# Layer 1's modulations move from the mixer into layer 0's values, summed by row on VectorE, with one more raw buffer and weight pair

## The chip, the cores and the metric

One core of a Trainium2 chip. The metric is the device time of one launch in microseconds, the median of several runs; lower is better.

## The reference, cut to what matters

A two-layer backbone over 256 latent tokens of 1024 features, with 256 context tokens in front. Each layer has a mixer and then a PEER expert layer, each with a normalisation that six modulation vectors of 1024 shift, scale and gate:

```python
c_act = jax.nn.silu(c)
for i in range(2):
    mod = (c_act @ ada_w[i] + ada_b[i]).reshape(bsz, 6, 1, 1024)
    sh1, sc1, g1, sh2, sc2, g2 = (mod[:, j] for j in range(6))
    h = rmsnorm(x, norm1_w[i]) * (1.0 + sc1) + sh1
    y = mixer_ab(h, h_c, ...) if i == 0 else fourier_mix(h) @ w_out_f
    x = x + g1 * y
    x = x + g2 * peer(rmsnorm(x, norm2_w[i]) * (1.0 + sc2) + sh2, ...)
return rmsnorm(x, final_norm_w)
```

`ada_w[i]` is 1024 x 6144, so a layer's modulations are one vector times 25 MB of weights. Layer 0's first two vectors are also needed for the context (with `c_ctx` in place of `c`). `peer` projects to queries (`wq`, 16 tiles), finds for each token and head the top 16 of 16,384 experts by two rounds of top-16 over keys, and sums `gate * gelu(h . u[e]) * v[e]`. The kernel computes all 16,384 activations with the table `u` (128 tiles of 128 experts), sets a dense weight matrix from the chosen experts, and multiplies with the table `v` (128 tiles).

## The kernel before

**Stages.** One program: the mixer of layer 0 (0 to about 440 us), `peer` of layer 0 (queries, the 128 `u` tiles with selection and weighting beside them, then the 128 `v` tiles), the Fourier mixer of layer 1 (about 1256 to 1290), `peer` of layer 1, the final norm.

**The weight stream.** `Stream` reads every large weight in one fixed order, as tiles of 128x1024 fp32 (512 KB). `loads` takes one of three raw buffers and starts the transfer on SyncE's queue. `cuts` splits each tile into a high part (a rounded copy in fp32r by ScalarE) and a low part (raw minus high, by VectorE), after which the raw buffer is free. The two parts of a tile are a pair; there are two pairs of the stream's own, and other stages lend theirs (two in the values, one in the `u` tiles). A 256-column product then takes three matmuls a block of 128: high x high, high x low and low x high, 24 matmuls to a tile.

**The modulations.** `modulations` in `mixer` computes both layers' vectors: six parts (two layers, three each), two halves, eight blocks of 128 input channels, 96 chunks of 512 KB. A chunk is loaded into one of six buffers for the first part, of two (`mraw`) for the others, and takes four fp32 matmuls, in which the activated condition (`cact`, 32 columns) is the stationary side and 256 chunk columns are the moving side; the trace has two records for each fp32 matmul. After a part, ScalarE copies the rows out (`mrow`), four transposes turn them into columns, and VectorE adds the bias. Layer 0's first part (16 chunks) must be there before the projections can start; its gates are needed at the mixer's end, and layer 1's vectors only after `peer` of layer 0.

**The rest of the mixer.** 29 projections (`products`, 17 of 512 columns and 12 of 256), at most three in flight, convolutions, attention, and a triangular inverse as 31 dependent steps on VectorE (`inverse`). When all projections are done, their buffer is set to zero by GpSimd (`zero`), the inverse is transposed into it (`blocks`), merged and scanned.

**Selection and weighting.** `select` runs top-16 on VectorE. `weigh` builds one-hot matrices on VectorE (four fp16 operations of 128x1024 for eight tokens), multiplies them on TensorE (fp16), and `spread` multiplies the result into the activations. Both run beside the `u` tiles. In `values` the weights are split (`weights`: ScalarE copies, VectorE subtracts, 128x512 per two tiles) and multiplied with the `v` pairs into four of the eight PSUM banks.

**The order.** The program is written by a planner. Each activity is a generator; `Lanes` keeps a clock for each engine, picks the generator that is ready first, and emits its next instructions. `took` is its price list and `landed` its guess at a transfer. The engines then run their own instructions in exactly that order, with semaphores between them. Prices so decide the order, not the time. `PACE` multiplies VectorE's prices in `select` (1.35) and `weigh` (1.1).

## Time and profile before

| what | value |
|---|---|
| median of 3 runs | 2119.27 us (2117.88 to 2119.61) |
| the profiled execution | 2115.18 us |
| its span, first to last instruction | 2113.4 us |
| mean granted TensorE clock | 0.989 of full speed |
| TensorE, VectorE, ScalarE busy | 2063.5, 1549.2, 1022.1 us |
| read from memory | 366.71 MB |

PE is TensorE's matmul, PEld its weight load, DVE VectorE, ACT ScalarE, POOL GpSimd, SPq SyncE's queue. Nearly all instructions stand at line 133, the planner's call, so groups are told apart by the names of their tiles: `raw` is a raw buffer, `pair`, `wide`, `h` and `wide_lo` hold parts of pairs at different times, `mraw` and `area` hold modulation chunks, `bank` is PSUM, `S` is the projections' input and later the inverse.

### The profile page before, as it was taken

The page shows a single profiled execution, that of the slowest core. Times are in us where ns is not written, and L with a number is a line of the kernel's source. Part 1 is how long each engine was busy: PE and PEld are TensorE (multiplying, and loading weights), DVE is VectorE, ACT ScalarE, POOL GpSimd, SP SyncE. Part 2 cuts the span into 40 slices and gives each one's busy share as a digit, 9 for nine tenths or more (in the row PEclk, how much of TensorE's full clock was granted, in tenths as well). Part 3 has the DMA queues.
Part 4 walks back from the last instruction along what each step waited for, and adds up shares of the span by engine and source line. Part 5 has one row for each costly group of instructions (what it writes and reads, how often), then busy time and mean ns, then how long its engine had stood idle before and what let it go on. Part 6 is the DMA issues. An engine that isn't in the chain of part 4 may idle for free.

```text
span 2113.4 us, 43065 instructions
## 1 busy us (share of the span) xinstructions
PE 2063.5 (98%) x17732; PEld 1933.9 (92%) x17732; DVE 1549.2 (73%) x3039; ACT 1022.1 (48%) x1542; POOL 82.8 (4%) x122
## 2 busy tenths in 40 slices
PE   7999989999999999999999999999999999999998
PEld 3566658989999999999999989999999999999997
DVE  3479978879998999565555556999899956555554
ACT  4443344155545444554444545554544455444453
POOL 3000023000000000000000000000000000000000
PEclk8999999999999999999999999999999999999999
DMA  7655671045565444665655543556544466666553
GB/s 300 213 180 169 232 240 38 1 133 180 189 198 170 142 149 151 198 212 196 192 195 194 193 160 116 172 190 199 170 141 149 150 199 211 195 194 193 196 192 118
DMA packets 102549, 370.65 MB, mean 175 GB/s; under 512 B 11696, under 2 KB 12976, under 8 KB 101968
## 3 DMA queue, kind: packets, MB, share of 16 engines
q1 hardware_dynamic: 102352, 367.90, 53.0%
q8 instruction: 138, 2.26, 0.4%
q14 instruction: 59, 0.48, 0.1%
HBM read 366.71 MB, written 1.15 MB: 174 GB/s over the span
## 4 chain that ended last, share of the span: by engine, by line
PE 79%; DVE 10%; DMA 6%; ACT 3%; issue 1%; POOL 0%; SPq 0%; POOLq 0%; ACTq 0%; DVEq 0%
PE bank L133 79%; DMA raw<-in_u_dram 3%; DVE wide_lo L133 3%; DVE pair L133 2%; DVE wide L133 2%; DMA mraw<-in_ada_w_dram 2%; DVE DD L133 1%; DVE area L133 1%; ACT pair L133 1%; DMA area<-in_ctx_dram 1%; ACT wide L133 0%; ACT DD L133 0%; DMA area<-in_ada_w_dram 0%; ACT bank L133 0%; DVE a L133 0%
## 5 line engine op out<-in xcount | busy, mean ns | idle before, releaser
L133 ACT ACTIVATE pair<-raw 128x1024 fp32r<-128x1024 f32 x376 | 399.1, 1062 | 435.2 <-PE bank L133 342.9
L133 DVE TENSOR_TENSOR pair<-raw,pair 128x1024 fp32r<-128x1024 f32 x376 | 458.1, 1219 | 182.8 <-ACT pair L133 167.1
L133 PE MATMUL bank<-h,pair 128*128 128x256 f32 x4464 | 557.4, 280 | 0.0
L133 PEld LDWEIGHTS bank<-h,pair 128*128 128x128 f32 x4464 | 528.8, 188 | 0.2 <-DVE pair L133 0.2
L133 PE MATMUL bank<-wide,pair 128*128 128x256 f32 (+1 forms) x3456 | 417.1, 277 | 0.0
L133 PEld LDWEIGHTS bank<-wide,pair 128*128 128x128 f32 x3456 | 405.4, 188 | 0.6
L133 PE MATMUL bank<-wide,h 128*128 128x256 f32 x2880 | 336.6, 276 | 0.0
L133 PEld LDWEIGHTS bank<-wide,h 128*128 128x128 f32 x2880 | 331.3, 188 | 0.0
L133 PE MATMUL bank<-h,wide 128*128 128x256 f32 x2160 | 264.5, 277 | 0.0
L133 PEld LDWEIGHTS bank<-h,wide 128*128 128x128 f32 x2160 | 253.7, 188 | 0.0
L133 DVE TENSOR_TENSOR h<-raw,h 128x1024 fp32r<-128x1024 f32 x120 | 147.0, 1225 | 140.1 <-ACT h L133 140.1
L133 ACT ACTIVATE h<-raw 128x1024 fp32r<-128x1024 f32 x120 | 127.4, 1062 | 161.8 <-PE bank L133 149.2
L133 PE MATMUL bank<-S,pair 128*128 128x256 f32 (+1 forms) x888 | 195.5, 362 | 4.2 <-POOL S L133 2.5
L133 PEld LDWEIGHTS bank<-S,pair 128*128 128x128 f32 x888 | 138.8, 199 | 52.3 <-issue 29.9
L133 ACT ACTIVATE DD<-bank 128x512 f32<-128x512 f32 (+25 forms) x284 | 107.6, 394 | 95.8 <-PE bank L133 92.8
L133 ACT ACTIVATE wide<-raw 128x1024 fp32r<-128x1024 f32 x90 | 95.6, 1062 | 106.7 <-PE bank L133 53.3
L133 DVE TENSOR_TENSOR wide<-raw,wide 128x1024 fp32r<-128x1024 f32 x90 | 109.3, 1214 | 2.3 <-ACT wide L133 2.0
L133 DVE TENSOR_TENSOR wide<-DD,wide 128x512 fp32r<-128x512 f32 x128 | 87.3, 684 | 8.3 <-ACT wide L133 8.2
L133 DVE TENSOR_TENSOR DD<-bank,DD 128x512 f32<-128x512 f32 (+13 forms) x84 | 42.3, 504 | 64.8 <-ACT bank L133 61.2
L133 DVE TENSOR_TENSOR wide_lo<-wide_lo,pT 128x1024 f16<-128x1024 f16 x128 | 85.9, 681 | 0.0
L133 ACT ACTIVATE wide<-DD 128x512 fp32r<-128x512 f32 x128 | 78.6, 615 | 9.5 <-PE bank L133 9.5
L133 POOL TENSOR_TENSOR wide_lo<-wide_lo 128x256 f32<-128x256 f32 x10 | 8.3, 834 | 1591.5 <-ACT wide_lo L133 1590.9
(242 smaller groups left out, 1893.7 us busy)
## 6 DMA issues: line engine op xcount, KB each, us to landing
raw<-in_u_dram SPq DMA_DIRECT2D x256, 512.0 KB, 3.5
raw<-in_v_dram SPq DMA_DIRECT2D x256, 512.0 KB, 4.3
mraw<-in_ada_w_dram SPq DMA_DIRECT2D x84, 512.0 KB, 4.2
raw<-in_wq_dram SPq DMA_DIRECT2D x32, 512.0 KB, 3.5
raw<-in_w_in_dram SPq DMA_DIRECT2D x29, 512.0 KB, 4.3
area<-in_ada_w_dram SPq DMA_DIRECT2D x12, 512.0 KB, 6.3
raw<-in_w_out_ab_dram SPq DMA_DIRECT2D x8, 512.0 KB, 4.5
raw<-in_w_out_f_dram SPq DMA_DIRECT2D x8, 512.0 KB, 3.5
```

The source lines that it names most:

```text
L133: return f(*args, **kw)
```

## The change

- Layer 1's 48 chunks leave `modulations` in the mixer, which keeps layer 0's three parts. Their weights are laid out anew (`ada_late`: vector, block of 128 input channels, 1024 outputs).
- They enter the weight stream among layer 0's 128 `v` tiles, two chunks for five tiles from the third tile on, in the order `ADA` of the vectors. They take raw buffers but no pair.
- A chunk is multiplied by its 128 condition values (one to a partition) and added into a 128x1024 accumulator `acc` by VectorE (`sum`): one `tensor_scalar`, then seven `scalar_tensor_tensor`. The first waits until the last vector's sum has been read.
- After eight chunks, TensorE sums over the partitions: eight fp32 matmuls with 128 columns of `acc` as the stationary side and one column of ones as the moving side (`Stream.modulations`). VectorE adds the bias.
- The stream has four raw buffers for three and three pairs of its own for two. The DMA scratch is set to 1024.
- The planner's prices change: `PACE` goes, three selection operations get their own constants, and an fp32r matmul costs n/2257 for n/2400.

```diff
--- before.py
+++ after.py
@@ -23,13 +23,10 @@
 NEG = -3.0e38
 GSC = 32768.0
 SKEW = 16
+ADA = 1, 0, 2, 4, 3, 5
 AHEAD = 6
 SUMMED = 6
 LN_EXP = "natural_log_exp_and_others"
-
-
-PACE = 1.35, 1.1
-
 
 EARLY = dict(cc=(KC, 2), ada_b=(2, 48), norm1=(2, KC), norm2=(2, KC), norm_f=(KC,))
 LATER = dict(conv=(12, 3), unit=(3,), unitw=(2,), headw=(2,), lam=(4,), ones64=(128,), tri=(128,), rot=(128,),
@@ -108,14 +105,12 @@
             elif args[2].dtype == F32:
                 d = n / 2400 if args[0].shape[0] == 32 else n / 600 if n >= 128 else 0.42
             else:
-                d = n / 2400
+                d = n / 2400 if args[2].dtype == F16 else n / 2257
         elif eng == "vector":
             d = n / (1920 if all(a.dtype == F16 for a in args[:3] if hasattr(a, "dtype")) else 960)
-            d = max(d + (0.115 if op.startswith("ma") else 0.07), 0.12)
+            d = max(d + dict(max=0.175, max_index=0.14, match_replace=0.25).get(op, 0.07), 0.12)
         else:
             d = n / (1200 if eng == "scalar" else 600) + 0.1
-        if self.cur and eng == "vector":
-            d *= self.cur.pace
         self.free[eng] = max(self.free.get(eng, 0.0), now) + d
         if self.cur:
             self.cur.t, self.cur.eng = self.free[eng], eng
@@ -138,7 +133,6 @@
 class Chain:
     def __init__(self, gen, t, low, ground):
         self.gen, self.t, self.low, self.ground, self.on, self.eng = gen, t, low, ground, [], None
-        self.pace = 1.0
 
     def wait(self, t, eng):
         if t > self.t:
@@ -200,11 +194,14 @@
 class Stream:
 
 
-    def __init__(self, c, pool, sources):
-        self.c, self.n, self.sources = c, 0, sources
+    def __init__(self, c, pool, sources, sums):
+
+        self.c, self.n, self.sources, self.sums = c, 0, sources, sums
+        self.order = [n for n in range(len(sources)) if n not in sums]
+        self.acc, self.summed, self.read = None, c.nc.events(6), c.nc.events(6)
         lanes = c.nc
-        self.raws = lanes.stock([c.t(pool, [128, 1024], tag=f"raw{i}") for i in range(3)])
-        self.parts = [lanes.stock(x) for x in zip(*(c.pair_tiles(pool, f"pair{i}") for i in range(2)))]
+        self.raws = lanes.stock([c.t(pool, [128, 1024], tag=f"raw{i}") for i in range(4)])
+        self.parts = [lanes.stock(x) for x in zip(*(c.pair_tiles(pool, f"pair{i}") for i in range(3)))]
         self.raw, self.tile = {}, {}
         self.loaded, self.cut = lanes.events(2, len(sources))
         self.begin = lanes.events(2)
@@ -226,6 +223,9 @@
         for n in range(len(self.sources)):
             yield self.loaded[n]
             raw, t = self.raw.pop(n)
+            if n in self.sums:
+                yield from self.sum(raw, t, *self.sums[n])
+                continue
             hi = yield from self.parts[0].take()
             yield t
             self.c.nc.scalar.activation(hi, raw, AF.Copy)
@@ -237,8 +237,36 @@
             self.cut[n].set()
             yield
 
+    def sum(self, raw, t, m, k):
+
+        nc, w = self.c.nc, self.c.cact[:, k, 0:1]
+        if k == 0 and m != ADA[0]:
+            yield self.read[ADA[ADA.index(m) - 1]]
+        yield t
+        if k == 0:
+            nc.vector.tensor_scalar(self.acc, raw, w, None, op0=OP.mult)
+        else:
+            nc.vector.scalar_tensor_tensor(self.acc, raw, w, self.acc, op0=OP.mult, op1=OP.add)
+        self.raws.give(raw)
+        if k == KC - 1:
+            self.summed[m].set()
+        yield
+
+    def modulations(self):
+
+        c, nc = self.c, self.c.nc
+        for m in ADA:
+            yield self.summed[m]
+            ps = yield from c.banks.take()
+            for j in range(8):
+                nc.tensor.matmul(ps[:, j:j + 1], self.acc[:, j * 128:j * 128 + 128], c.ones[:, :1], start=True, stop=True)
+            self.read[m].set()
+            yield
+            nc.vector.tensor_tensor(c.mod[1][:, 0, m * 8:m * 8 + 8], ps[:, :8], c.adab[:, 1, m * 8:m * 8 + 8], op=OP.add)
+            c.banks.give(ps)
+
     def next(self):
-        n = self.n
+        n = self.order[self.n]
         self.n += 1
         yield self.cut[n]
         return self.tile.pop(n)
@@ -255,14 +283,14 @@
 class Ctx:
 
 
-    def __init__(self, tc, es, sources):
+    def __init__(self, tc, es, sources, sums):
         self.tc, self.nc = tc, Lanes(tc.nc)
         self.n = 0
         self.const = es.enter_context(tc.tile_pool(name="const", bufs=1))
         self.share = es.enter_context(tc.tile_pool(name="share", bufs=1))
         banks = es.enter_context(tc.tile_pool(name="banks", bufs=1, space=PSUM))
         self.banks = self.nc.stock([self.t(banks, [128, 512], tag=f"bank{i}") for i in range(8)])
-        self.stream = Stream(self, self.const, sources)
+        self.stream = Stream(self, self.const, sources, sums)
 
     def t(self, pool, shape, dt=F32, tag=None, **k):
         self.n += 1
@@ -566,11 +594,11 @@
         flight = lanes.stock(range(3))
 
 
-        parts = [(i, p) for i in range(2) for p in range(3)]
+        parts = [(0, p) for p in range(3)]
         modk = events(len(parts))
         mrow = new([128, 512], tag="mrow")
         mraw = [new([128, 4, 256], tag=f"mraw{i}") for i in range(2)]
-        mraw = [[view(S3, 4, 256, at=i * 1024) for i in range(4)] + mraw] + [mraw] * 5
+        mraw = [[view(S3, 4, 256, at=i * 1024) for i in range(4)] + mraw] + [mraw] * 2
 
         there = lanes.event()
         fetched = {n: lanes.event() for n in (6, 16)}
@@ -1407,6 +1435,9 @@
         a1 = c.t(dp, [128, 1024], F16, tag="a1")
         x = c.scaled
         squares, c.squares = c.squares, Squares(c, layer == 0)
+        if layer == 0:
+            stream.acc = c.t(dp, [128, 1024], tag="acc")
+            lanes.add(stream.modulations())
         late = {}
 
         def region(j, n):
@@ -1521,7 +1552,7 @@
 
         def select(tb):
 
-            lanes.cur.pace, lanes.cur.low = PACE[0], "vector"
+            lanes.cur.low = "vector"
             w = Scratch(region(80 + 12 * tb, 12))
             rep, cand, rep2 = w(128), w(112), w(112)
             tv = w(256).rearrange("p (h s a) -> p h s a", h=8, s=2)
@@ -1617,7 +1648,6 @@
 
 
             yield pk
-            lanes.cur.pace = PACE[1]
             oa, bh, ob = late["onehots"][i]
             for g in range(i, NT // 8, 2):
                 i1, i2, hi, lo = (pT[:, n, g * 8:g * 8 + 8].rearrange("p (g t) -> p g t", g=4).unsqueeze(2)
@@ -1741,8 +1771,16 @@
     with ExitStack() as es:
         tiles = lambda *names: [a[i] for a in names for i in range(a.shape[0])]
         layers = [tiles(A["wq"][i], A["u"][i], A["v"][i]) for i in range(2)]
-        c = Ctx(tc, es, tiles(A["w_in"], A["w_out_ab"]) + layers[0] + [A["dft"]] + tiles(A["w_out_f"])
-                + layers[1])
+
+        chunks = [(m, k) for m in ADA for k in range(KC)]
+        sources, sums = tiles(A["w_in"], A["w_out_ab"]) + layers[0][:-128], {}
+        for j, v in enumerate(layers[0][-128:]):
+            sources.append(v)
+            while len(sums) < len(chunks) and 2 * (j - 2) >= 5 * len(sums):
+                m, k = chunks[len(sums)]
+                sums[len(sources)] = m, k
+                sources.append(A["ada_late"][m, k])
+        c = Ctx(tc, es, sources + [A["dft"]] + tiles(A["w_out_f"]) + layers[1], sums)
         nc = c.nc
 
         def const(name):
@@ -1815,7 +1853,8 @@
     a["x"], a["ctx"] = feature_major(i["x"][0]), feature_major(i["ctx"][0])
     a["cc"] = con(np.stack([i["c"][0], i["c_ctx"]], -1).reshape(8, 128, 2).transpose(1, 0, 2))
 
-    a["ada_w"] = con(i["ada_w"].reshape(2, 8, 128, 3, 4, 2, 256).transpose(0, 3, 5, 1, 2, 4, 6)).reshape(2, 3, 2, 8, 128, 1024)
+    a["ada_w"] = con(i["ada_w"][:1].reshape(1, 8, 128, 3, 4, 2, 256).transpose(0, 3, 5, 1, 2, 4, 6)).reshape(1, 3, 2, 8, 128, 1024)
+    a["ada_late"] = con(i["ada_w"][1].reshape(8, 128, 6, 1024).transpose(2, 0, 1, 3))
     a["ada_b"] = con(i["ada_b"].reshape(2, 48, 128).transpose(2, 0, 1))
     a["norm1"], a["norm2"] = by_channel(i["norm1_w"]), by_channel(i["norm2_w"])
     a["norm_f"] = con(i["final_norm_w"].reshape(8, 128).T)
@@ -1877,7 +1916,7 @@
     from concourse.bass_utils import run_bass_kernel_spmd
 
     host = arrays({k: np.asarray(v) for k, v in inputs.items()})
-    nc = bacc.Bacc("TRN2", target_bir_lowering=False, num_devices=1)
+    nc = bacc.Bacc("TRN2", target_bir_lowering=False, num_devices=1, dynamic_dma_scratch_size=1024)
     A = {k: nc.dram_tensor(f"in_{k}_dram", v.shape, mybir.dt.from_np(v.dtype), kind="ExternalInput").ap()
          for k, v in host.items()}
     out = nc.dram_tensor("out_0_dram", (128, KC, NT), F32, kind="ExternalOutput").ap()
```

## Rows read from the trace of the kernel before

**Rows 1.** The page's busy time by engine: busy us (share of the span) and instructions.

```profile
PE 2063.5 (98%) x17732; PEld 1933.9 (92%) x17732; DVE 1549.2 (73%) x3039; ACT 1022.1 (48%) x1542; POOL 82.8 (4%) x122
```

**Rows 2.** Busy us (instructions) of each engine in stages, then clock, DMA share, GB/s.

```profile
180.00:246.00 66.00, 61.49 (x422) 41.63 (x419) 63.84 (x98) 19.80 (x36) 0.00 (x0) 0.95 0.67 221
246.00:272.00 26.00, 25.64 (x197) 16.19 (x196) 25.79 (x41) 12.19 (x27) 7.59 (x5) 1.00 0.74 249
272.00:302.00 30.00, 26.33 (x177) 16.39 (x175) 16.69 (x45) 15.59 (x36) 6.96 (x11) 0.89 0.73 245
302.00:331.00 29.00, 25.57 (x275) 17.05 (x272) 25.58 (x53) 15.39 (x36) 7.40 (x2) 1.00 0.57 183
...
684.00:828.00 144.00, 141.77 (x1389) 138.26 (x1388) 135.94 (x218) 70.24 (x134) 0.00 (x0) 1.00 0.44 143
...
900.00:1246.00 346.00, 346.00 (x3052) 346.00 (x3051) 194.25 (x191) 169.39 (x192) 0.00 (x0) 1.00 0.60 195
...
1543.00:1674.00 131.00, 128.64 (x1259) 125.58 (x1259) 123.92 (x197) 63.54 (x120) 0.00 (x0) 1.00 0.45 145
```

**Rows 3.** The chain that ended last, 0 to 440 us: start, length, what.

```profile
250.34 4.34 DMA mraw<-in_ada_w_dram
...
323.24 4.06 DMA mraw<-in_ada_w_dram
```

**Rows 4.** The stages again, instructions on the modulation chunks (mraw) alone.

```profile
180.00:246.00 66.00, 12.68 (x156) 3.18 (x152) 0.95 0.67 221
246.00:272.00 26.00, 6.39 (x80) 1.57 (x80) 1.00 0.74 249
272.00:302.00 30.00, 6.17 (x72) 1.46 (x72) 0.89 0.73 245
302.00:331.00 29.00, 5.77 (x76) 1.42 (x72) 1.00 0.57 183
```

**Rows 5.** Timeline of PE, 246 to 332 us: start, length, instruction [idle before, releaser].

```profile
276.72 1.08 PE L133 MATMUL bank<-mraw,cact 128*32 128x256 f32 x8 [2.53 <-DMA mraw<-in_ada_w_dram]
...
279.18 1.05 PE L133 MATMUL bank<-ident,mrow 128*128 128x128 f32 x4
...
290.83 0.64 PE L133 MATMUL bank<-mraw,cact 128*32 128x256 f32 x8 [0.43 <-DMA mraw<-in_ada_w_dram]
291.40 2.10 PE L133 MATMUL bank<-S,pair 128*128 128x256 f32 x16
...
297.45 0.64 PE L133 MATMUL bank<-mraw,cact 128*32 128x256 f32 x8 [0.61 <-DMA mraw<-in_ada_w_dram]
```

**Rows 6.** Timeline of all engines, 1243 to 1262 us: the sums of squares.

```profile
1261.06 0.61 PE L133 MATMUL bank<-ones,wide_lo 128*128 128x1 f32 x4 [1.34 <-POOL wide_lo L133]
...
1261.53 0.71 PE L133 MATMUL bank<-pair,h 128*128 128x512 f32 x2
```

**Rows 7.** Groups of instructions, 900 to 1246 us: busy, mean ns, idle before, releasers.

```profile
L133 DVE TENSOR_TENSOR pair<-raw,pair 128x1024 fp32r<-128x1024 f32 x68 | 83.3, 1225 | 76.6 <-ACT pair L133 76.6
...
L133 ACT ACTIVATE pair<-raw 128x1024 fp32r<-128x1024 f32 x67 | 71.2, 1062 | 91.5 <-PE bank L133 88.3 <-DMA raw<-in_v_dram 1.7 <-DVE pair L133 1.3
```

**Rows 8.** Groups of instructions by shape on DVE, whole span.

```profile
L133 DVE SCALAR_TENSOR_TENSOR wide_lo<-wide_lo,sm 128x512 f32<-128x512 f32 x8 | 6.0, 747 | 0.1
```

**Rows 9.** DMA issues, 900 to 1246 us: count, KB each, us to landing.

```profile
raw<-in_v_dram SPq DMA_DIRECT2D x127, 512.0 KB, 4.3
```

**Rows 10.** DMA issues, 246 to 331 us.

```profile
mraw<-in_ada_w_dram SPq DMA_DIRECT2D x26, 512.0 KB, 4.0
raw<-in_w_out_ab_dram SPq DMA_DIRECT2D x5, 512.0 KB, 6.0
```

**Rows 11.** Groups of instructions on PE, 684 to 828 us.

```profile
L133 PE MATMUL bank<-wide_lo,a 128*128 128x128 f16 x211 | 18.0, 220 | 0.3 <-DVE wide_lo L133 0.2
L133 PE MATMUL bank<-wide_lo 128*128 128x128 f16 x208 | 17.7, 220 | 1.9 <-DVE wide_lo L133 1.7
```

**Rows 12.** Timeline of all engines, 684 to 740 us: fp16 weight loads.

```profile
692.06 0.46 PEld L133 LDWEIGHTS <-wide_lo 128*128 128x128 f16 x8
```

## The prediction

> **What bounds the kernel now.** I read the page's busy times first: TensorE is busy for 98% of the span [rows 1]. A matmul's recorded end is modelled, so that share doesn't prove that nothing else limits; I cut the span into stages and looked in each for an engine without idle time [rows 2]. The reader should see four kinds of stage. From 180 to 272 us (the mixer's triangular inverse) VectorE is busy 63.8 of 66 and 25.8 of 26 us. From 272 to 331 us nothing is full: VectorE has 16.7 of 30, then 25.6 of 29 us. In layer 0's weighting stage (684 to 828) and layer 1's (1543 to 1674) VectorE has 135.9 of 144 and 123.9 of 131 us. In the values (900 to 1246) TensorE is full and VectorE has 194 of 346 us. The chain of waits then says what ends last in the loose stage: from 250 to 327 us it goes eight times through the landing of a modulation chunk, first and last shown [rows 3]. TensorE runs in program order, so a late chunk holds up the projections behind it.
>
> **The mixer's side (gain).** Layer 1's 48 chunks leave. By the weight loads, eight records to a chunk, 152 + 80 fall between 180 and 272 us, 72 between 272 and 302, 72 between 302 and 331 [rows 4]: 29, 9 and 9 chunks, one before. A chunk holds TensorE from 290.83 to 291.40, 0.57 us [rows 5]; the three sets of transposes go too, 1.05 us for the one shown.
> - 180 to 272 us: 29 x 0.57 = 16.5 us of TensorE, but VectorE is idle for only 2.4 us [rows 2]. I take 1 us.
> - 272 to 302 us: 9 x 0.57 = 5.1, a transpose row 1.0, and visible waits for chunks of 2.53 + 0.43 + 0.61 = 3.6 us [rows 5]: 9.7 us, with VectorE idle for 13.3 [rows 2]. Some of the freed time will meet activations on ScalarE instead; I take 8.
> - 302 to 331 us: 5.1 + 1 us of TensorE, VectorE idle for 3.4. I take 3.
>
> Sum 12 us. Below, 0: VectorE's work is all still there and the stage could be paced by it. Above, VectorE's whole idle time from 246 to 331 us, 0.2 + 13.3 + 3.4 = 17 us. I stay nearer to the upper end because the loose stretch is the one in which the chain names the chunks. SyncE's queue in the mixer loses 48 loads, and those behind them start earlier; the chain there names no other load, so I give that nothing.
>
> **The values' side (loss).** Six times, 8 one-column matmuls of 128x128 fp32 enter TensorE's queue among layer 0's values, where TensorE is full [rows 2]; 48 in all. The nearest row is the sum of squares: four records (two to a matmul) start at 1261.06 and the next matmul at 1261.53, so 0.47 us for two [rows 6], 0.235 each: 11.3 us. Bounds: 0.1134 us per record at the values' own pace (346.0/3052, [rows 2]) gives 10.9; and if the recorded 0.61 us for two were not overlapped, 14.6. Before each set TensorE must wait for the last VectorE sum. Nothing shows this wait; the nearest is the 1.34 us for GpSimd's sum in the same rows. So 0 to 6 x 1.34 = 8 us; I take 0.4 each, 2.5 in all, since the emission order puts the set behind the sum's planned end. Sum +13.8 us, from 10.9 to 22.6.
>
> The sums themselves: a 128x1024 subtraction takes 1.225 us [rows 7], a 128x512 scalar_tensor_tensor 0.747 [rows 8], so a 1024-wide sum lies between 1.2 and 1.5 us. 48 x 1.2 = 58 us on a VectorE that has 152 idle [rows 2]: nothing, while values keep being cut ahead. Without that cover each would cost its 1.2 us, 58 us. The first product of a set also waits until TensorE has read the old sum; behind it in VectorE's queue stand the next value's subtraction and the weights' split. Chunks come 2.5 values apart, 2.5 x 24 x 0.1134 = 6.8 us, so TensorE has read long before: nothing. If not, TensorE would be waiting for values behind that subtraction and I'd see it there. The six additions of the bias, which wait on VectorE for their set, have the same cover, and four of the eight banks are free for the sets.
>
> The loads: each chunk is issued on SyncE's queue between two value loads and waits there for a free raw buffer; value loads queue up behind it. A value now needs, in three buffers, 3 x 2.72 = 8.16 us per turn (24 x 0.1134 = 2.72), of which ScalarE waits 88.3/67 = 1.3 us for TensorE's release [rows 7]: 6.85 needed. A chunk skips ScalarE's 1.06 us [rows 7]: about 5.7. Mean of five values and two chunks 6.5, plus 0.5 for a fuller VectorE queue (an estimate, under half a subtraction) is 7.0. Four buffers and seven loads in 5 x 2.72 + 0.47 = 14.07 us allow 4 x 14.07/7 = 8.04. It holds as long as landing, now 4.3 us [rows 9], stays under 5.3. The traffic grows from 195 GB/s [rows 2] by 1.4 to 270; at 249 GB/s in the mixer [rows 2] the chunks landed in 4.0, but five other loads took 6.0 [rows 10]. I take nothing, with the rest as a rival.
>
> By the Trainium skill (DMA: Bandwidth & Descriptors, Latency and other measured facts), HBM access takes 0.2 us on average but 2 us at high load. By it alone landing would reach 6.1 us and the values grow by some 30 us, an estimate from that page; the 4.0 us of the chunks at 249 GB/s so far speaks against it [rows 10].
>
> **Buffers and the planner (gain).** The fourth raw buffer and third pair can take stalls out of the two weighting stages. From 684 to 828 us TensorE has 1389 matmuls, 419 of them fp16 [rows 2, 11]; eight fp16 loads take 0.46 us [rows 12], so 970 x 0.1134 + 419 x 0.0575 = 134 us of 144: 10 us of stall. Layer 1, with 1259 in the same mix: 121.5 of 131, 9.5 us. VectorE is idle for only 8 and 7 us there, but its work need not all lie there, as the values' stages have room. I take half, 9 us in both; from 0 to 19. A loss isn't excluded: the order on VectorE is the planner's, which now prices a one-hot operation 10% lower (no pace of 1.1) and a split matmul 6% higher (2257 for 2400). It may put more one-hot work ahead of a subtraction; I bound this by as much stall again as one stage has, 10 us.
>
> The smaller DMA scratch costs nothing: every row of the transfer list is issued by SyncE, none by GpSimd.
>
> **Sum.** -12 - 9 + 13.8 = -7.2 us. The profiled execution took 2115.2 us, 2113.4 of span and 1.8 around it; it would be 2108.0. The median of the runs is 4.1 us above it, so 2119.3 - 7.2 = 2112.
>
> **Rivals.**
> - VectorE keeps the mixer: its inverse, convolutions and softmax sums are all there, and the freed TensorE time runs into them. For: 180 to 272 us is full. Against: 13.3 us idle right after [rows 2]. Mixer -2, rest as forecast: +2.8, 2122.
> - The raw buffers bound the values (slower). It decides at a landing of 5.3 us; at the 6.0 us of [rows 10] a turn needs 8.7, seven loads 15.2 for 14.07 us, and 24 such groups cost 28 us: 2119.3 - 7.2 + 28 = 2140. Against it: 4.0 us at nearly the same traffic. (This is the way the skill's page would have it.)
> - The new order hurts the weighting stages: +9.5 for -9, so -12 + 9.5 + 13.8 = +11.3, 2131. For: VectorE has almost no room there. Against: two buffers more give TensorE a longer stock.
> - All of it comes: mixer -17, both stalls gone -19, values +11.3: -24.7, 2095. Against: VectorE would have to run without idle time for 85 us.
>
> **How the numbers follow.** A kernel this long can be told from no change at about 0.2%, 4.2 us: faster is below 2115, slower above 2123.5. Chances: forecast 0.42 (its own range 2105 to 2119), VectorE keeps the mixer 0.24, raw buffers 0.12, worse order 0.10, everything 0.12. Faster: 0.42 x 0.8 + 0.12 = 0.46. Slower: 0.12 + 0.10 + a tenth of the second case, and a little for a longer wait at the six sets: 0.25. The rest, 0.29, the same. The range leaves out the buffers' case and half of the best one, 0.18: 2097 to 2132.
>
> **What would show it.** Right: the last matmul on a modulation chunk ends near 180 us, and the transposes and copies that end here at 331 us end some 12 us earlier; layer 0's values hold six sets of 16 short records, each about 1.9 us with under 1 us of idle time before; ScalarE's casts there still wait for TensorE, not for the transfers; the weighting stages shrink by 4 to 5 us each. Wrong: VectorE full up to the end of those copies with no shorter mixer; casts of values waiting for transfers landing above 5.3 us; TensorE waiting on VectorE at the sums for more than 1.3 us; or a weighting stage longer than before.

## The result and the profile after

The changed kernel takes 2136.44 us (median of 6 runs, 2130.73 to 2139.3), the kernel before 2118.15 us beside it (6 runs, 2109.87 to 2119.61): ratio 1.0091 [1.0069, 1.0112], 18 us slower. I had forecast 2112, with a range up to 2132. Time and direction were wrong. The profiled execution took 2139.3 us, with a span of 2137.5. It is the slowest of the six, so the profiles compared below lie 24 us apart and not 18. Ratios, here and below, are of means, and the times are medians.

To find where the time went I read in each trace the start of the same five instructions: the first query product, the first product on a value tile, Fourier's first product, layer 1's first value product, and the first output transfer. The lengths between them, in us:

| stretch | before | after | difference |
|---|---|---|---|
| mixer | 463.3 | 444.8 | -18.5 |
| layer 0: queries, `u` tiles, selection, weighting | 443.5 | 455.5 | +12.0 |
| layer 0's values | 350.1 | 367.6 | +17.5 |
| Fourier, and layer 1 up to its values | 495.6 | 509.1 | +13.5 |
| layer 1's values and the end | 354.9 | 354.3 | -0.6 |
| sum | 2107.4 | 2131.3 | +23.9 |

The mixer gave more than the 12 us forecast, and the values cost 17.5 for 13.8. What broke the sum are the two stretches with selection and weighting: I had counted 9 us of gain, and they lost 25.5.

The page's busy times of the changed kernel, against [rows 1]:

```profile
PE 2065.6 (97%) x17432; PEld 1958.3 (92%) x17432; DVE 1599.0 (75%) x3104; ACT 1023.4 (48%) x1539; POOL 93.9 (4%) x122
```

300 matmuls fewer, and yet 2.1 us more of TensorE's time; VectorE has 50 us more, where the sums alone are 42 x 1.284 + 6 x 0.744 = 58 (I did not trace the 8 us between). The same stages as in [rows 2], and one more, 503 to 624 us:

```profile
180.00:246.00 66.00, 57.50 (x323) 46.58 (x321) 66.00 (x106) 25.21 (x43) 3.47 (x2) 0.91 0.22 72
246.00:272.00 26.00, 20.15 (x92) 15.66 (x93) 26.00 (x42) 11.34 (x26) 8.02 (x4) 0.76 0.29 89
272.00:302.00 30.00, 27.33 (x134) 17.85 (x134) 23.54 (x62) 15.96 (x40) 12.22 (x10) 0.73 0.29 82
...
503.00:624.00 121.00, 111.10 (x949) 110.42 (x948) 114.90 (x387) 58.58 (x67) 0.00 (x0) 0.96 0.52 170
684.00:828.00 144.00, 144.00 (x1391) 142.22 (x1389) 125.39 (x190) 73.95 (x125) 0.00 (x0) 1.00 0.47 155
900.00:1246.00 346.00, 343.75 (x2984) 342.95 (x2983) 236.27 (x236) 160.06 (x184) 0.00 (x0) 1.00 0.78 259
1543.00:1674.00 131.00, 131.00 (x1298) 128.93 (x1297) 124.95 (x200) 68.59 (x125) 0.00 (x0) 1.00 0.44 146
```

The reader should see three things. The weighting stages (684, 1543) have lost their idle time: TensorE is busy for 144.00 and 131.00 us, where it had 141.77 and 128.64. The values, with 259 GB/s for 195, leave TensorE idle for 2.25 us. And a new gap stands in a stage that the prediction never priced, the selection, top-16 beside the `u` tiles: 949 matmuls in 121 us. The same stretch of the kernel before:

```profile
503.00:624.00 121.00, 121.00 (x1064) 121.00 (x1063) 115.51 (x403) 62.17 (x75) 0.00 (x0) 1.00 0.57 189
```

115 matmuls are missing after. The chain of waits after, from 500 us (start, length, what):

```profile
499.96 3.00 PE bank L128 x26
...
502.99 1.07 ACT wide L128
...
504.24 1.23 DVE pair L128
505.47 0.52 DVE DD L128 x4
...
507.14 1.21 DVE wide L128
508.35 0.46 DVE DD L128 x3
```

`DD` is the selection's work, `pair` and `wide` are subtractions of weight tiles. From 503 us on the chain runs on VectorE, selection and subtractions in turn. What TensorE itself waits for from 503 to 624 us is a single thing (us in total, times, longest):

```profile
PE bank L128 <- DVE DD L128: 9.9, 3, 4.9
```

It waits three times for the selection, and never for a subtraction. Windows of 20 us of the changed kernel show where TensorE stands still:

```profile
500.00:520.00 20.00, 20.00 (x178) 20.00 (x177) 19.07 (x75) 10.86 (x12) 0.00 (x0) 1.00 0.51 171
520.00:540.00 20.00, 16.50 (x146) 16.30 (x144) 19.62 (x54) 11.33 (x14) 0.00 (x0) 0.96 0.49 162
540.00:560.00 20.00, 17.57 (x126) 17.28 (x127) 18.41 (x67) 6.18 (x7) 0.00 (x0) 0.78 0.51 163
560.00:580.00 20.00, 20.00 (x179) 20.00 (x178) 19.28 (x73) 9.47 (x12) 0.00 (x0) 1.00 0.55 181
...
620.00:640.00 20.00, 16.18 (x138) 15.98 (x139) 18.76 (x32) 7.11 (x12) 0.00 (x0) 0.91 0.49 161
```

The holes lie where the selection's fp16 block ends, at 540 and 622 us, once for each half of the tokens. The first one on TensorE's timeline (idle time before it in brackets), a subtraction on VectorE's, and the block in VectorE's groups from 520 to 540 us:

```profile
533.62 2.88 PE L128 MATMUL bank<-h,wide 128*128 128x256 f32 x24
541.44 0.69 PE L128 MATMUL bank<-ident,DD 128*128 128x128 f32 x2 [4.94 <-DVE DD L128]
541.78 0.56 PE L128 MATMUL bank<-h,pair 128*128 128x256 f32 x1
543.33 0.47 PE L128 MATMUL bank<-ident,DD 128*128 128x128 f32 x1 [0.99 <-DVE DD L128]
543.46 4.83 PE L128 MATMUL bank<-h,pair 128*128 128x256 f32 x21
```

```profile
534.92 1.22 DVE L128 TENSOR_TENSOR pair<-raw,pair 128x1024 fp32r<-128x1024 f32 x1
```

```profile
L128 DVE SCALAR_TENSOR_TENSOR DD<-DD 128x256 f16<-128x256 f16 (+1 forms) x18 | 6.2, 404 | 0.1
```

`ident,DD` are the three transposes of the selection's result. TensorE stops at 536.50 us, although the next tile's subtraction ended at 536.14: its 24 matmuls are ready, but the transposes stand ahead of them in TensorE's queue, and the result that they transpose is not there yet. So the hole is a question of the place of the transposes. Behind it the granted clock is 0.78 from 540 to 560 us: 126 matmuls take 17.57 us, and 21 of them 4.83, which is 0.23 each for 0.1134. From 503 to 624 us TensorE is idle for 9.9 us (121 less 111.10); the stretch lost 15.0 us in all (below). I put the other 5 down to this clock: 126 matmuls at 0.1134 would take 14.3 us, so 3.3 of the 5 lie behind the first hole.

For the experiments I use one more number, the **excess** of a stretch: its length less what its matmuls take (0.1134 us for an fp32r record, 0.0575 for fp16, as in the prediction, 0.117 for others). In layer 0, before and after:

| stretch | before | after |
|---|---|---|
| selection (50 us after the first query product to the first one-hot operation) | -0.1 | 15.0 |
| weighting (from there to the values) | 11.3 | 8.1 |
| values | 1.4 | 7.7 |

### The profile page after: what moved, and what is told of

It is laid out like the page before. It is cut to its first block, busy times and chain, and to the rows that moved or that the text cites. A ratio compares the mean times of both kernels' runs of the same rounds, so it can differ in the third digit from the quotient of the medians.

```text
span 2137.5 us, 42709 instructions
## 1 busy us (share of the span) xinstructions
PE 2065.6 (97%) x17432; PEld 1958.3 (92%) x17432; DVE 1599.0 (75%) x3104; ACT 1023.4 (48%) x1539; POOL 93.9 (4%) x122
## 4 chain that ended last, share of the span: by engine, by line
PE 80%; DVE 14%; DMA 3%; issue 2%; ACT 1%; POOL 1%; POOLq 0%; SPq 0%; DVEq 0%; ACTq 0%
PE bank L128 80%; DVE DD L128 4%; DVE pair L128 3%; DVE wide L128 3%; DVE area L128 2%; DMA raw<-in_ada_late_dram 1%; ACT pair L128 1%; DMA raw<-in_v_dram 0%; DMA mraw<-in_ada_w_dram 0%; POOL area L128 0%; DVE sm L128 0%; DMA area<-in_ada_w_dram 0%; DVE bq L128 0%; DVE wide_lo L128 0%; DMA x<-in_x_dram 0%
## 5 line engine op out<-in xcount | busy, mean ns | idle before, releaser
L128 DVE TENSOR_TENSOR pair<-raw,pair 128x1024 fp32r<-128x1024 f32 x422 | 513.2, 1220 | 165.5 <-ACT pair L128 146.6
L128 PE MATMUL bank<-h,pair 128*128 128x256 f32 x4992 | 617.4, 281 | 0.0
L128 PEld LDWEIGHTS bank<-h,pair 128*128 128x128 f32 x4992 | 592.3, 189 | 0.0
L128 PE MATMUL bank<-wide,pair 128*128 128x256 f32 (+1 forms) x4008 | 482.6, 278 | 1.9 <-DVE wide L128 1.8
L128 PEld LDWEIGHTS bank<-wide,pair 128*128 128x128 f32 x4008 | 470.8, 189 | 2.4 <-DVE wide L128 2.3
L128 PE MATMUL bank<-wide,h 128*128 128x256 f32 x2328 | 274.0, 277 | 0.3 <-ACT wide L128 0.2
L128 PEld LDWEIGHTS bank<-wide,h 128*128 128x128 f32 x2328 | 269.3, 188 | 0.7 <-ACT wide L128 0.4
L128 PE MATMUL bank<-h,wide 128*128 128x256 f32 x1632 | 209.1, 281 | 0.0
L128 PEld LDWEIGHTS bank<-h,wide 128*128 128x128 f32 x1632 | 197.0, 191 | 0.0
L128 PEld LDWEIGHTS bank<-S,pair 128*128 128x128 f32 x888 | 138.1, 199 | 44.4 <-issue 17.5
L128 ACT ACTIVATE DD<-bank 128x256 f32<-128x256 f32 (+17 forms) x270 | 107.3, 406 | 69.9 <-PE bank L128 62.4
```

Of the source, the lines that this page charges most:

```text
L128: return f(*args, **kw)
```

## The experiments

Theory P: the new prices cost the time, by the order that they make. Theory B: it is the buffers, which let the stream run ahead and crowd VectorE. Ratios are to the kernel before, run beside; excess and lengths come from one profiled execution each, which lies up to 5.6 us from its median (e8), so that a few us between two rows say nothing.

| run | time, us | ratio | mixer | excess: selection, weighting, values | values | Fourier and layer 1 |
|---|---|---|---|---|---|---|
| after | 2136.44 | 1.0091 [1.0069, 1.0112] | 444.8 | 15.0, 8.1, 7.7 | 367.6 | 509.1 |
| e1_old_prices | 2114.95 | 0.9999 [0.9985, 1.0013] | 443.3 | 0.2, 10.5, 4.5 | 364.4 | 501.2 |
| e2_new_prices_alone | 2162.86 | 1.0217 [1.0189, 1.0244] | 477.3 | 15.2, 9.2, 1.4 | 350.1 | 513.1 |
| e3_buffers_alone | 2122.96 | 1.0033 [1.0021, 1.0046] | 462.1 | 0.3, 13.5, 0.1 | 348.7 | 498.5 |
| e4_fewer_buffers | 2196.55 | 1.0382 [1.0364, 1.0399] | 453.9 | 15.3, 8.8, 50.0 | 409.8 | 511.3 |
| e5_old_vector_prices | 2110.08 | 0.9976 [0.9959, 0.9993] | 441.0 | 1.2, 9.9, 4.8 | 364.6 | 495.5 |
| e6_old_matmul_price | 2115.72 | 1.0000 [0.9986, 1.0014] | 447.7 | 2.9, 9.2, 5.9 | 365.9 | 496.8 |
| e7_higher_pace | 2116.88 | 1.0016 [1.0003, 1.0030] | 447.7 | 0.3, 11.9, 3.3 | 363.1 | 498.8 |
| e8_measured_prices | 2108.57 | 0.9962 [0.9951, 0.9974] | 442.5 | 0.6, 8.3, 5.1 | 364.9 | 492.1 |
| e9_chunks_earlier | 2103.36 | 0.9939 [0.9918, 0.9959] | 440.1 | 0.9, 8.3, 0.8 | 358.7 | 496.4 |
| e10_measured_prices_alone | 2129.36 | 1.0065 [1.0041, 1.0090] | 476.0 | 1.3, 9.1, 1.7 | 350.3 | 496.7 |
| e11_one_product_a_set | 2100.20 | 0.9928 [0.9899, 0.9957] | 444.2 | 0.9, 8.4, 6.5 | 356.5 | 491.0 |
| e12_search_price | 2110.67 | 0.9972 [0.9953, 0.9990] | 442.5 | 5.9, 8.2, 3.6 | 363.5 | 495.4 |
| e13_fused_price | 2131.60 | 1.0068 [1.0038, 1.0099] | 445.8 | 10.8, 9.4, 8.9 | 368.9 | 502.1 |

**Prices or buffers.** Three runs split the change.

e1 is the changed kernel with `took` and `PACE` of before:

```diff
-                d = n / 2400 if args[2].dtype == F16 else n / 2257
+                d = n / 2400
-            d = max(d + dict(max=0.175, max_index=0.14, match_replace=0.25).get(op, 0.07), 0.12)
+            d = max(d + (0.115 if op.startswith("ma") else 0.07), 0.12)
+        if self.cur and eng == "vector":
+            d *= self.cur.pace
```

> The changed kernel with all of the planner's old prices (the pace of 1.35 and 1.1, the old constants, 2400 for the split matmul); chunks, sums, fourth raw buffer and third pair stay. Theory P, the new prices cost the time: layer 0's stretch from the first query product to the first value product, 443.5 us before and 455.5 after, falls back to 445 or below, layer 1's stretch from the Fourier mixer's first product to the first value product (495.6 before, 509.1 after) to 497 or below; the whole is near 2137 - 25 = 2112 us. Theory B, the deeper buffers cost it (the planner lets weight tiles run further ahead and fills VectorE's queue otherwise): both stretches stay at 455 and 509, the whole at 2136.

e2 is the reverse, the kernel before with the new prices alone.

> The kernel before with the new prices alone: chunks stay in the mixer, three raw buffers, two pairs. Theory P: layer 0's stretch grows from 443.5 to 455 us, layer 1's from 495.6 to 509, the whole by 20 to 26 us to 2140. Theory B: the whole stays at 2118.

e3 is the kernel before with four raw buffers, three pairs and the smaller DMA scratch: `range(3)` to `range(4)`, `range(2)` to `range(3)`.

> The kernel before with the fourth raw buffer, the third pair and the smaller DMA scratch, old prices, chunks in the mixer. Theory P: the stalls of the weighting stages shrink as predicted, 5 to 9 us faster, 2110. Theory B: both stretches grow by 12 us each, 2142.

P holds. With the old prices the selection's excess falls from 15.0 to 0.2 us, and the changed kernel is level with before; the new prices alone bring it into the kernel before (15.2), the buffers alone don't (0.3). B falls: the buffers cost 0.33%, not 0.9. Two forecasts made under P missed: e3's gain of 5 to 9 us didn't come (its two stretches are 446.2 and 498.5 us, each some 3 longer than before), and e1's second stretch fell to 501.2 us, not 497.

e2 lost more than the 20 to 26 us expected, as its mixer is 14 us longer too. The traces say which price does that. Up to the first query product, e2 and e10 have the same instructions in the same order on TensorE, VectorE, ScalarE and GpSimd; so have the changed kernel, e5 and e8, which differ in VectorE's prices alone. Before and e2 part at VectorE's 54th instruction. In the mixer no VectorE price that the change touches is used, so the price of the split matmul is left: with the chunks there, 2257 for 2400 costs 13 to 14 us. With the chunks gone it makes no clear difference (443.3, 447.7 and 447.7 us with the old price, 440.1 to 445.8 with the new). The three mixers with the old price (e1, e6, e7) also run one order, so 4 us between mixers are noise.

**Which price.** e5 puts back VectorE's prices and `PACE` alone, e6 the matmul's price alone, and e7 is e1 with `PACE = 1.7, 1.3`.

> The changed kernel with VectorE's old prices (pace 1.35 and 1.1, old constants) and the new price of the split matmul (2257). Theory V, the lower VectorE prices do the harm: the whole falls to 2115, as with all prices old, the two weighting stretches to 443 and 501 us. Theory M, the dearer matmul does it: the whole stays near 2136, the stretches at 455 and 509. If both share it, 2122 to 2130.

> The changed kernel with the old price of the split matmul (2400) and VectorE's new prices. Theory V: stays near 2136 or gets worse, since a cheaper matmul against cheap VectorE work leaves the ratio at 1.35/1.06 below the old one. Theory M: 2115.

> The changed kernel with all old prices and the pace raised from 1.35 and 1.1 to 1.7 and 1.3. Theory V read as a scale (dearer selection and weighting means fewer stalls): the stalls that are left in the weighting, 10 us a layer, shrink to 5, and the whole is 2105. If VectorE's real work bounds the weighting whatever the order: 2115, as with the old prices. If the values then wait for the later weights: above 2115.

Either old price brings nearly all of it back, and a higher pace gives nothing on top. So no single price is to blame; it is the share of selection to tiles in the planner's clock. The trace says how far that clock is off. One step of top-16 over 128 elements on VectorE, from the kernel before:

```profile
501.33 0.08 DVE L133 MATCH_VALUE_LOAD DD<-DD 128x8 f32 x1
501.40 0.29 DVE L133 FIND_INDEX8 DD<-DD 128x8 uint32<-128x128 f32 x1
501.60 0.28 DVE L133 MAX8 DD<-DD 128x8 f32<-128x128 f32 x1
501.92 0.09 DVE L133 MATCH_VALUE_LOAD DD<-DD 128x8 f32 x1
502.00 0.29 DVE L133 FIND_INDEX8 DD<-DD 128x8 uint32<-128x128 f32 x1
502.20 0.07 DVE L133 MATCH_VALUE_LOAD DD<-DD 128x8 f32 x1
502.25 0.28 DVE L133 MATCH_REPLACE8 DD<-DD 128x128 f32<-128x128 f32 x1
502.57 0.29 DVE L133 MAX8 DD<-DD 128x8 f32<-128x128 f32 x1
```

With each search's and replacement's value load that is 1.6 us (501.33 to 502.94, where the next subtraction starts). The new prices make it 2 x 0.308 + 2 x 0.148 + 0.383 = 1.295. The index search is the worst: 0.148, because its 8 results are counted and not the 128 elements that it reads. The other one is the fp16 fused operation, `scalar_tensor_tensor` with 256 elements, here beside an fp16 `tensor_tensor` in the changed kernel's timeline:

```profile
536.05 1.42 DVE L128 SCALAR_TENSOR_TENSOR DD<-DD 128x256 f16<-128x256 f16 x4
537.51 1.23 DVE L128 TENSOR_TENSOR DD<-DD 128x2048 f16<-128x2048 f16 x1
```

Four take 1.42 us; they start 0.335 us apart, and one alone lasts 0.417, as long as a `tensor_tensor` over 512 fp16 elements (0.424). The price puts both operations at 1920 elements a us: 0.203 for the fused one. By the Trainium skill (VectorE: DVE Perf Modes, What auto-detection actually checks) the engine takes its doubled mode if every tensor is 16-bit with step 1 or -1. One operand here is a broadcast value, with step 0 inside, and the rows agree with that; but no run takes the broadcast out, so it can as well be the operation.

So the planner believes the selection to be done sooner than it is: the fp16 block alone, 18 operations (two of them over 128 elements), is priced 16 x 0.203 + 2 x 0.137 = 3.5 us and takes 6.2. It then gives TensorE the transposes of the result too early. How early can be counted in the traces, as the number of split matmuls between the first query product and the first transpose, with what TensorE waits at layer 0's transposes:

| run | split matmuls ahead of the first transpose | wait at the transposes, us | selection's excess, us |
|---|---|---|---|
| after | 720 | 9.9 | 15.0 |
| e13_fused_price | 748 | 7.2 | 10.8 |
| e5_old_vector_prices | 808 | 0.7 | 1.2 |
| e12_search_price | 816 | 2.7 | 5.9 |
| e6_old_matmul_price | 824 | 1.9 | 2.9 |
| e8_measured_prices | 856 | 0.3 | 0.6 |
| e1_old_prices | 900 | 0 | 0.2 |

In these seven runs TensorE waits for nothing else in that stretch, and in layer 1 the waits are nearly the same (9.6 us in after, 0.3 in e8). The later the transposes stand, the less TensorE waits; only e5 is out of line, and there the selection is done sooner (by 101 us after the first query product, in e12 at 103). A cheaper selection and a dearer matmul both move the transposes forward, which is why either old price mends it. With three raw buffers and two pairs (e2 and e4) TensorE waits 7.8 and 7.6 us at the transposes and another 2.7 and 3.1 for subtractions: there the stock of cut tiles runs out as well. In e5, with as many selection operations, TensorE has no such hole (120.72 us busy of 121, 503 to 624).

e8 mends both prices, e10 does the same in the kernel before (its new prices and these lines), e12 and e13 mend one each:

```diff
+            if op == "max_index":
+                n = args[2].shape[-1]
-            d = n / (1920 if all(a.dtype == F16 for a in args[:3] if hasattr(a, "dtype")) else 960)
+            d = n / (1920 if op != "scalar_tensor_tensor" and all(a.dtype == F16 for a in args[:3] if hasattr(a, "dtype"))
+                     else 960)
```

> The changed kernel with two of its VectorE prices mended to what the trace shows: the index search counts its 128 source elements and not the 8 of its output (0.148 to 0.273 us; in the trace a search and its load take 0.28), and scalar_tensor_tensor in fp16 counts at 960 elements a microsecond, not 1920 (0.203 to 0.337 for 256; six in a row took 2.09). If theory V holds because these two are too cheap: the selection's stalls go, the stretches fall to 443 and 501, the whole to 2115. If not the accuracy but a high level as such is needed (a margin over the real cost): stays above 2125.

> The kernel before with the two mended prices and the other new ones: chunks in the mixer, three raw buffers, two pairs. If wrong prices alone made the selection stall, the stretches are 443 and 495 us, not 457.6 and 513.1 as with the new prices alone. The mixer, which took 463.3 us with old prices and 477.3 with the new ones alone, tells whether the same two prices touch it: neither operation is used there in fp16 or as a search, so it should stay at 477; the whole then 2132. If it returns to 463: 2117.

> The changed kernel with one price mended: the index search is counted by the 128 elements that it reads, 0.273 us for 0.148. The fp16 fused operation stays priced at twice its speed. If the search's price alone put selection ahead of the subtractions, the stretch from the first top-16 step to the first one-hot operation returns from 15 us of stall to under 3, and the time falls from 1.009 of before to about 1.000. If it is the sum of all prices that must pass a point (a step of 1.57 us priced below about 1.33), this one alone also passes it, with the same times. If the fused operation is the cause, stall and time stay as they are, 15 us and 1.009.

> The changed kernel with the other price mended: the fp16 fused operation (256 elements) at 0.337 us for 0.203; the index search stays at 0.148. If the search's price alone is the cause, 15 us of stall in the selection's stretch and 1.009 of before remain. If the fused operation is the cause, or the sum of all prices is what counts (no matter which is mended), the stall falls under 3 us in each layer and the time to about 1.000.

With both mended the excess is 0.6 and the kernel is 0.4% faster than before. The search alone gives back 9.1 of 15.0 us of layer 0's excess and 13.7 of the 17.0 that e8 gains in Fourier and layer 1; the fused operation gives back 4.2 and 7.0. e10 does the same without the move: its two stretches are back at 443.2 and 496.7 us, and its 0.65% over before is its mixer's, 12.7 us. A single cause and a point that the sum of prices must pass, as I had it in the expectations, are both wrong: the excess falls with each price, the search being the larger. Nor must each price be right by itself, as e5's old, paced prices do nearly as well (0.9976, and the intervals overlap). The stretch from 503 to 624 us in e12, then in e8:

```profile
503.00:624.00 121.00, 119.27 (x1029) 118.88 (x1028) 115.24 (x386) 62.03 (x71) 0.00 (x0) 0.99 0.57 184
```

```profile
503.00:624.00 121.00, 121.00 (x1068) 121.00 (x1067) 116.74 (x384) 63.79 (x74) 0.00 (x0) 1.00 0.59 192
```

VectorE is about as busy as in the changed kernel (114.90), in another order: 44 subtractions for 39 there, and 23 fused operations over 256 elements for 32. TensorE gets 1068 matmuls through for 949. The chain of e8 from 500 to 520 us is TensorE alone. From 640 to 890 us it is so in e8 and in the changed kernel alike; e8's row:

```profile
640.00 250.09 PE bank L131 x2380
```

**The values.** e4 is the changed kernel with three raw buffers and two pairs.

> The changed kernel with three raw buffers and two pairs, new prices, chunks among the values. Theory P: the weighting stretches stay at 455 and 509 us or get longer; the values, 367.6 us with four raw buffers, are bound by three (a turn of 7 us against 14.07 x 3/7 = 6.0) and grow by some 50 us; the whole 2180 or more. Theory B: the stretches fall to 444 and 496, and the whole is 2160.

The values take 409.8 us, 42 more than after for the 50 expected, and the other two stretches stay as P had it (456.7 and 511.3). The values hold 128 + 48 = 176 loads, so a raw buffer's turn is 3 x 409.8/176 = 6.99 us, the 7.0 of the prediction; four buffers allow 4 x 359.8/176 = 8.2 (359.8 is what the matmuls need). The fourth buffer is what makes the move possible, as far as e4 shows it: it takes the third pair away too, but ScalarE's casts there wait for transfers before all else (186 of 225 us). Still the changed kernel isn't free of waits there. Its groups on ScalarE, 900 to 1246 us, against [rows 7]:

```profile
L128 ACT ACTIVATE pair<-raw 128x1024 fp32r<-128x1024 f32 x73 | 77.4, 1060 | 130.1 <-DMA raw<-in_v_dram 91.2 <-PE bank L128 32.2 <-DVE h L128 3.8
```

The casts now wait for transfers. The landing isn't late, as the DMA issues after show (900 to 1262 us; 4.3 in [rows 9]):

```profile
raw<-in_v_dram SPq DMA_DIRECT2D x123, 512.0 KB, 4.5
raw<-in_ada_late_dram SPq DMA_DIRECT2D x47, 512.0 KB, 4.4
```

So the transfers start late, for lack of a free buffer: SyncE's queue waits 63 of the 100 us from 900 on for VectorE's last reading of a raw buffer. TensorE's timeline after shows the place, near the start, and a set of sums that costs no idle time:

```profile
930.97 9.16 PE L128 MATMUL bank<-wide,pair 128*128 128x256 f32 x64 [1.84 <-DVE wide L128]
...
960.92 1.84 PE L128 MATMUL bank<-ones,acc 128*128 128x1 f32 x16
962.62 8.25 PE L128 MATMUL bank<-wide,pair 128*128 128x256 f32 x68
```

e9 is e8 with the chunks begun 22 `u` tiles earlier, one for three tiles:

```diff
-        sources, sums = tiles(A["w_in"], A["w_out_ab"]) + layers[0][:-128], {}
+        sources, sums = tiles(A["w_in"], A["w_out_ab"]) + layers[0][:-128 - 22], {}
-            while len(sums) < len(chunks) and 2 * (j - 2) >= 5 * len(sums):
+            while len(sums) < len(chunks) and j >= 3 * len(sums):
```

> The kernel with measured prices, with one chunk to three weight tiles, begun 22 tiles before the end of layer 0's activations, in place of two to five among the values alone. If the 5 us of layer 0's values beyond their matmuls (364.9 us against 359.8) are the raw buffers running dry while the first chunks come in, they shrink to 2 or less; the values' stretch is 361 us and the whole 3 to 4 us faster, ratio 0.994. If they are waits of the sets for VectorE's sums, they stay: 365 us. If the chunks disturb the end of the weighting, layer 0's weighting stretch grows beyond 441 us.

e11 is e8 with one product in a set instead of eight; seven eighths of the sums over the partitions are left out, and one column stands for all.

> The kernel with measured prices; of the eight one-column products of each of the six sets only the first is made, and its column stands for all eight, so layer 1's modulations are not the reference's. 42 products fewer. If one costs TensorE 0.23 us on a full queue, layer 0's values shrink from 364.9 us by 9.7, to 355. If TensorE waits at each set for the sum all the same, by less: 358 or more.

e9's values have 0.8 us of excess for 5.1, and are 6.2 us shorter than e8's; it is the fastest complete kernel here, 0.61% faster than before. The casts' waits for transfers shrink, and TensorE is busy for 346.00 of 346 us; ScalarE's group in e9:

```profile
L131 ACT ACTIVATE pair<-raw 128x1024 fp32r<-128x1024 f32 x75 | 79.7, 1062 | 106.9 <-PE bank L131 79.6 <-DMA raw<-in_v_dram 21.8 <-DVE pair L131 3.2
```

Whether the earlier start or the slower pace of the chunks does it was not tried. e11's 42 products fewer make the values 8.4 us shorter than e8's, 0.20 each for the 0.235 forecast; with a few us of noise between two profiles, the sets' price was about right.

## Why the prediction was wrong, step by step

**The step that failed: "Buffers and the planner (gain)".** It has two halves. The new prices were taken up as a risk for one-hot work in the weighting stage, bounded by "as much stall again as one stage has, 10 us", with a chance of 0.10 for the rival made from it (+9.5, 2131). The two stretches lost 25.5 us, and not there but in the selection before, where TensorE had no excess at all (-0.1 us), so that no bound taken from an existing stall could hold it. Nor is the wait the one feared: TensorE doesn't wait for a subtraction behind one-hot work but at the selection's own transposes, 9.9 us in layer 0 and 9.6 in layer 1. The prediction quoted only two of the price changes (the pace of 1.1, and 2257 for 2400) and left out those of the selection (the pace of 1.35 and three new constants), which make a fused operation of some 0.34 us cost 0.203 for 0.274. That the rival's 2131 lies near the 2136.44 measured is luck: its mechanism is another. Without the prices the change is worth nothing (e1, 0.9999), with mended ones it gains (e8, 0.9962).

The other half, 9 us from two more buffers, was mis-sized. Of the "10 us of stall" little was stall: TensorE is idle for 2.2 of the 144 us [rows 2]. In e8 the chain from 640 to 890 us is TensorE alone, and 8.3 us of excess remain. TensorE's timeline before shows what they are, where fp16 products stand between split ones:

```profile
684.09 0.63 PE L133 MATMUL bank<-wide_lo,a 128*128 128x128 f16 x8
684.53 0.72 PE L133 MATMUL bank<-h,pair 128*128 128x256 f32 x4
685.09 0.63 PE L133 MATMUL bank<-wide_lo,a 128*128 128x128 f16 x8
```

Four split matmuls hold TensorE from 684.53 to 685.09, 0.56 us for 4 x 0.1134 = 0.45, with no idle time. In e8's stage such stretches of split matmuls between fp16 ones come 62 times and take 0.11 us too long each (median), 9.8 us in all; the fp16 blocks give 1.2 back. That is the 8.3. The prediction's count of matmuls had no term for it. So at most 11.3 - 8.3 = 3 us were to be had in layer 0, and the changed kernel did get them (8.1). With the old prices (e1 10.5, e3 13.5) even that didn't show.

**The mixer, right and under-sized.** Forecast -12, measured -18.5 to its end (-15.4 at the scan's first product, 391.39 to 376.02 us). The 1 us for 180 to 272 us was right: the inverse's last step on VectorE starts at 265.7 us for 267.4. The term that was too small is the 8 us for 272 to 302, as the projections that filled this stretch are done before it: the zeroing, which comes behind the last of them, begins at 277.9 us for 298.9, and the inverse's first copy on ScalarE at 292.8 for 313.6. The last modulation chunk is done at 141 us, where I had said 180, as the summary of that tile after shows:

```profile
L128 PE MATMUL bank<-mraw,cact x288: 379/379/404, 16.0 to 140.9; 128*32 128x256 f32 x144
```

The rival by which VectorE keeps the mixer (2122) falls: it is full from 180 to 272 us in both kernels, but its work behind comes earlier (from 272 to 302 us it is busy for 23.54 us, for 16.69 in [rows 2]), and the last of the inverse's copies on ScalarE starts at 316.6 us for 332.8.

**The values, right in kind.** Forecast +13.8, measured +17.5, and +14.3 in e1. The sets took 1.70 us each from their start to the next product, 10.2 for 11.3 forecast. The wait before a set, 2.5 us forecast, is zero: no set has idle time before it. The sums take 1.284 us, within the 1.2 to 1.5 forecast, and VectorE had the room (236 of 346 us):

```profile
L128 DVE SCALAR_TENSOR_TENSOR acc<-raw,cact,acc 128x1024 f32<-128x1024 f32 x42 | 53.9, 1282 | 47.4 <-DMA raw<-in_ada_late_dram 47.4
```

**The raw buffers.** The turn of 7.0 us was right (e4), but I priced only the steady state. The rest of the +17.5 is a shortage that begins with the values; e9 takes it out. The rival's mechanism didn't happen: landing stayed at 4.5 us with 259 GB/s, below the 5.3 at which it decides. The Trainium skill's figure (DMA: Bandwidth & Descriptors, Latency and other measured facts), 2 us for memory access at high load, would have put it at 6.1, by the prediction's estimate; the 4.5 us measured don't bear that out here.

## What to carry to other kernels

Where a planner's prices set the order, a changed price is a change of the program: hold every price that the diff touches against that instruction's own row, and sum them over a unit of work (here a top-16 step, priced 1.295 and taking 1.6 us). Where one engine's work is priced too low, the planner puts what depends on it too early into another engine's queue; that engine, in program order, stops there with ready work behind, and it does so where it had no stall to begin with. A bound taken from today's stalls doesn't cover that. Excess of a stage over its matmul count is not stall until a wait in the chain carries it.

## What the runs showed of the hardware that I had not expected

One hole costs twice: after 4.94 us without work TensorE's granted clock is 0.78 from 540 to 560 us, so part of that time is at the 1.2 GHz level, and 126 matmuls take 17.57 us, 0.139 each, for 0.112 in a full window (179 in 20 us). With the chunks gone the same happens in the mixer: TensorE has gaps, and its clock is 0.76 and 0.73 from 246 to 302 us, for 1.00 and 0.89 in [rows 2]. The mixer gained all the same.

Switching between fp16 and split products costs TensorE time without any idle time: 0.56 us for four matmuls that take 0.45 among their own kind. An fp16 `scalar_tensor_tensor` with a broadcast operand takes 0.417 us over 256 elements, as long as `tensor_tensor` does over 512 (0.424).
